# One weight sum of every second gate block on VectorE, a new order of weight loads, and term stores from ScalarE's queue

## The chip, the core and the metric

The kernel runs on one core of a Trainium2 chip. Five engines run side by side, each in its own program order: TensorE (PE) multiplies, VectorE (DVE) and ScalarE (ACT) do elementwise work, GpSimd (POOL) and SyncE (SP) issue transfers. A transfer is issued on the queue of one engine and carried by the core's 16 DMA engines. The metric is the time of one execution in microseconds (us) on the device; lower is better.

## The reference

One decoder block over 512 tokens of width 2048 in float32: an RMSNorm, one input projection, two attention mixers, an output projection, and a SwiGLU feed-forward layer with a hidden width of 5632. The change touches only the feed-forward layer, whose core is

```python
hn2 = rmsnorm(h, norm2_g[l])
h = h + (jax.nn.silu(hn2 @ w_gate[l]) * (hn2 @ w_up[l])) @ w_down[l]
return rmsnorm(h, final_g)
```

## The kernel before

**Blocks and products.** The feed-forward layer is done in 64 blocks, numbered here as in the code: 44 gate blocks (0 to 43), one for each 128 hidden columns, and 20 down blocks (44 to 63). The order stands in the table `sched`. A block holds four weight matrices of 128x1024 floats, A11, A21, A22 and A12 (512 KB each), and is computed with a seven-product scheme in place of eight plain products. The products are P1 to P7, and PE takes them in the order P1, P5, P6, P2, P7, P3, P4 (block 0 has an order of its own). Their weights are: P1 A11; P5 Y = A21 + A22; P6 Y + A11; P2 A12; P7 X = A21 + A11; P3 Y + A11 + A12; P4 A22. Signs are folded into the operands on the other side (`term`: B11, T1, T2, B21, T3, B22, T4). So four matrices are read, and four sums are formed.

**Who forms the sums.** Y and X were formed by transfers: SP loads A21 into a buffer, and then POOL issues a second transfer (line 135 of the kernel before) that reads the other matrix and adds it to the buffer. The sums of P6 and P3 are formed in Y's buffer by DVE (`comb`, line 804). For the blocks in the tuple `OWN`, DVE also forms X: A21 is loaded plainly and `comb("A11", "X")` adds A11. Before the change `OWN` held blocks 43 and 44 alone.

**Splits.** Each weight is split into a high and a low part in a narrower format before PE can use it: ACT writes the high part (`Job.first`, line 173) and DVE the low part (`Job.second`, line 176) into one of three buffers `w`. A product is 8 weight tiles with three matmuls each (lines 1015, 1016, 1017): high part by high operand, high part by low operand, low part by high operand. The low part of a weight is thus first needed by the third matmul of its product.

**Ticks.** All work is written out by hand in ticks. A tick is half a product (12 matmuls); a block has 14. For a product that PE starts at tick n, its `comb` is written at tick n-5, its high split at n-4 and its low split at n-3; within an odd tick low splits stand ahead of sums. Within a block, counted from its start, P2's low split stands at tick 3, P7's high split at 4, P7's low split and P3's sum at 5, P3's high split at 6 and P3's low split at 7. A tick is only a place in each engine's program: an engine that waits delays everything written behind it.

**Buffers and loads.** Raw weights have six buffers of 512 KB. `loads` lists all loads in order, and `load_to` issues the next one as soon as `release` has freed a buffer, so the order of the list and the places of the releases set when each load starts. A block frees its buffers at tick -1 (A11, after P6's sum), 5 (X after P7's low split, A12 after P3's sum), 7 (Y) and 9 (A22). Where DVE forms X, A11 is needed longer and is freed at tick 3.

**Evacuation and stores.** `gate` moves products out of PSUM, and `pair_terms` makes from two gate blocks the seven terms of the hidden layer, in `even1` to `even3` behind an even block and `odd1` to `odd3` behind an odd one (high parts by ACT, low parts by DVE, into the staging area in `ah` and `al`). ACT's copy of P5 (`g5`, line 1129) goes into the buffer `ft` that the previous block's `u` leaves, so it waits for the last low part that `pair_terms` makes of that `u`. After each odd block `store` writes the staged terms to DRAM, in two transfers of 896 KB, which happens while the next even block runs. They come back by `fetch` (line 1074) in the down blocks.

**Alignment.** P1's weights of every fourth block (1, 5, 9, ... and block 2) are put at another offset of the buffer `w` (`even`).

Of the kernel before, what the change touches and what calls it, by code (L numbers as in the profile page):

```python
# [11 lines left out]
F32 = mybir.dt.float32  # L12
# [10 lines left out]
FB = FF // 128  # L23
# [1 line left out]
PAIRS = 20  # L25
NCH = PAIRS // PH
FC = 2 * PAIRS
OWN = (FB - 1, FB)
PASS2 = tuple(8 * b + a for a in range(8) for b in range(2))
EPS = 1e-6  # L30
BIG = 1e30
# [44 lines left out]
def block_kernel(ctx: ExitStack, tc: tile.TileContext, xt, wst, wdn, smalls, wg, w2c, bias, ident_in, out):  # L76
# [3 lines left out]
    pe, act, dve, pool_e, sp = nc.tensor, nc.scalar, nc.vector, nc.gpsimd, nc.sync  # L80
# [27 lines left out]
    n_units = next(u for u, d in enumerate(units) if d[0] == "quad")  # L108
    loads = [(u, wst[u], None) for u in range(n_units)]
    for u in range(n_units, len(units), 4):  # L110
        a11, a21, a22, a12 = (wst[u + q] for q in range(4))
        loads += [((u, "A11"), a11, None), ((u, "Y"), a21, a22), ((u, "A12"), a12, None), ((u, "X"), a21, None if (u - n_units) // 4 in OWN else a11),
                  ((u, "A22"), a22, None)]
    loads += [(("fin", k), wdn[2 * k:2 * k + 2].rearrange("n p c -> p n c"), None) for k in range(KB // 2)]
    pools = {"raw": wp}

# [71 lines left out]
    k = 2 * units.index(("out", 0, 1))  # L188
# [43 lines left out]
    def later(n, f):  # L232
        i = len(lag)
        while i and lag[i - 1][0] > pos["half"] + n:
            i -= 1
        lag.insert(i, (pos["half"] + n, f))
# [113 lines left out]
    for k in range(KB):  # L350
        x = xc.pop(k)
# [137 lines left out]
    def evac(p, tag, scale=None, keep=False):  # L489

        t = tmp()
        if scale is None:
            dve.tensor_tensor(t, p, r1, op=OP.mult)
        else:
            dve.scalar_tensor_tensor(t, p, scale, r1, op0=OP.mult, op1=OP.mult)
        ph, pl = (MH, ML) if tag[0] == "k" else (WH, WL)
        h = placed(kvq(tag), S, ph, tag=tag + "h", name=tag + "h")
        l = placed(kvq(tag), S, pl, tag=tag + "l", name=tag + "l")
        act.activation(h, t, AF.Copy)
        dve.tensor_tensor(l, t, h.bitcast(F32), op=OP.subtract)  # L500
        return (h, l, t) if keep else (h, l)
# [212 lines left out]
    def proj_block(upto=None):  # L714
        return ps.tile([128, 512], F32, tag="proj", name="pp", bufs=2)
# [40 lines left out]
    for j in range(NH):  # L756
# [5 lines left out]
        p = proj_block()  # L762
# [8 lines left out]
        p = proj_block()  # L771
# [3 lines left out]
        p = proj_block()  # L775
        for half in range(2):
            in_unit(p, half)
        k = evac(p, "ka")
        v = V()
        queue.append(Att("dil", q, k, v, ba, None, {}, True, True, head_done(j, 0)))  # L780
        p = proj_block()
# [15 lines left out]
    def quad_jobs(u, order, even, own):  # L797

        def raw(k):
            return lambda: raws[u, k]  # L800

        def comb(k, to="Y", last=True):
            def f():
                dve.tensor_tensor(raws[u, to], raws[u, to], raws[u, k], op=OP.add)  # L804
                if last:
                    release((u, k))
            return f

        r = {"P1": Job(raw("A11"), even=even), "P5": Job(raw("Y")), "P6": Job(raw("Y"), prep=comb("A11", last=not own)),
             "P2": Job(raw("A12")), "P7": Job(raw("X"), prep=comb("A11", "X") if own else None, done=((u, "X"),)),  # L810
             "P3": Job(raw("Y"), prep=comb("A12"), done=((u, "Y"),)), "P4": Job(raw("A22"), done=((u, "A22"),))}
        return [r[p] for p in order]
# [9 lines left out]
    for i, (kind, f, m) in enumerate(sched):  # L822
        for job in quad_jobs(n_units + 4 * i, ORDER if i else ORDER0, i == 2 or i % 4 == 1, i in OWN):
            job.n = now_at // 2
# [16 lines left out]
    def out_unit(half, tag="proj"):  # L841
        p = ps.tile([128, 512], F32, tag=tag, name="pab", bufs=2)
        c = 8 - 8 * half
        run_unit([(p, ah[:, c + k, :], al[:, c + k, :], k == 0, k == 7) for k in range(8)])
        return p
# [60 lines left out]
    for nb in range(2, KB):  # L906
        while "hs" not in rest and (nb == 4 and not idle() or nb == 2 and (queue or cur["s"])):
            step()
        p = out_unit(1, ("proj", "sc", "t")[nb // 2 % 3])
# [87 lines left out]
    for i in range(KB):  # L997
        nb = PASS2[i]
        p = out_unit(0)
# [47 lines left out]
    def sub(o, a, b):  # L1047
        dve.tensor_tensor(o, a, b, op=OP.subtract)

    stage = [a[:, 12:16, :].rearrange("p a b -> p (a b)") for a in (ah, al)]  # L1050
    scr = [scp.tile([128, 14 * 1024], F32, name=f"scr{c}") for c in range(NCH)]

    def st_high(k, n, src):
        act.activation(stage[0][:, 256 * k:256 * k + 256 * n], src, AF.Copy)

    def st_low(k, n, src):
        c = slice(256 * k, 256 * k + 256 * n)
        dve.tensor_tensor(stage[1][:, c], src, stage[0][:, c].bitcast(F32), op=OP.subtract)

    def stt(o, a, b):  # L1060
        dve.scalar_tensor_tensor(o, a, -1.0, b, op0=OP.mult, op1=OP.subtract)

    def store(i):

        for x in range(2):
            d = scr[i // PH].rearrange("p (x n s c) -> p x n s c", x=2, n=7, s=PH)[:, x, :, i % PH, :]
            sp.dma_start(d, stage[x][:, :1792].bitcast(F32).rearrange("p (n c) -> p n c", c=256))

    NAMES = ("B11", "T1", "B21", "B22", "T2", "T3", "T4")

# [5 lines left out]
    def pair_terms(f, u):  # L1076

        def even1():
            st["v"] = ps.tile([128, 512], F32, tag="o", name="v")
            act.activation(st["v"][:, HI], u[:, HI], AF.Copy)  # L1080

        def even2():
            sub(u[:, HI], u[:, LO], u[:, HI])
            st_high(0, 2, u)

        def even3():
            act.activation(st["v"][:, LO], u[:, HI], AF.Copy)
            st_low(0, 2, u)

        def odd1():  # L1090
            st_high(2, 2, u)
            v = st["v"]
            sub(v[:, HI], u[:, HI], v[:, HI])
            stt(v[:, LO], v[:, LO], u[:, HI])

        def odd2():
            st_low(2, 2, u)
            v = st["v"]
            st_high(4, 2, v)
            stt(u[:, LO], v[:, LO], u[:, LO])  # L1100

        def odd3():
            st_high(6, 1, u[:, LO])
            st_low(4, 2, st["v"])
            st_low(6, 1, u[:, LO])

        for i, g in enumerate((odd1, odd2, odd3) if f % 2 else (even1, even2, even3)):
            later(i, g)
        if f % 2:
            later(5, lambda: store(f // 2))  # L1110

    def hidden(f, u):
        h, l = ah[:, 12 + f % PH, :], al[:, 12 + f % PH, :]
# [86 lines left out]
    for kind, f, m in sched:  # L1200
        order = ORDER if kind == "d" or f else ORDER0
        for i, name in enumerate(order):
            product(kind, f, m, name)
            if kind == "d":
                down(m, name)
                k = 7 * m + i
# [179 lines left out]
```

## Time and profile before

| | us |
|---|---|
| median of three runs | 2176.89 (2173.27 to 2178.32) |
| the profiled execution | 2174.71 |
| its span, first to last instruction | 2172.9 |
| start of gate block 0 | 837.0 |
| start of gate block 2 | 881.6 |
| start of down block 44 | 1718.0 |
| last down block over, last steps | from 2113.4 |

Times inside the profile count from the span's start, which is 1.8 us shorter than the execution. The median of the runs lies 2.2 us above the profiled execution. The gate blocks take 881 us of the span. Over blocks 2 to 43 (881.6 to 1718.0) DVE is busy for 633.6 us of 836.4, ACT for 419.6, and the DMA engines for 80% of the time. A matmul is shown with a modelled length of 0.28 us though the next one starts 0.11 to 0.12 us later, so PE looks busy nearly always; its pace is read from the starts.

### The profile page before, as it was taken

How to read it: one execution, taken by the hardware profiler on the slowest of the kernel's cores; microseconds unless marked ns; L12 is line 12 of the kernel's file. 1: busy time of each engine (PE TensorE's matmuls, PEld its weight loads, DVE VectorE, ACT ScalarE, POOL GpSimd, SP SyncE). 2: the span in 40 equal slices, each digit the busy share in tenths (PEclk: the TensorE clock that was granted, in tenths of full speed). 3: DMA queues.
4: the chain of work that ended last, by engine and by line, in shares of the span. 5: the costliest groups of instructions: out<-in, count | busy, mean ns of one | idle time of the engine just before them, and what ended most of it. 6: DMA issues, size and time to landing. Idle time of an engine off the chain costs nothing.

```text
span 2172.9 us, 37846 instructions
## 1 busy us (share of the span) xinstructions
PE 2146.5 (99%) x15296; PEld 2004.1 (92%) x15296; DVE 1542.1 (71%) x2510; ACT 1013.1 (47%) x1702; POOL 147.0 (7%) x172
## 2 busy tenths in 40 slices
PE   9999999999999999999999999999999999999997
PEld 8888888888888888999999999999999999999997
DVE  6755565356667588777877777777777767787875
ACT  6544444344444255554545554454545433333345
POOL 0000000000000000000000000000000000000003
PEclk9999999999999999999999999999999999999999
DMA  6442222322225335778878888787788889899862
GB/s 224 152 132 80 84 77 78 100 80 80 75 74 178 104 97 132 215 215 245 231 221 231 236 248 240 200 261 223 209 248 236 282 264 292 267 292 287 268 193 78
DMA packets 143534, 403.60 MB, mean 186 GB/s; under 512 B 12288, under 2 KB 50816, under 8 KB 143360
## 3 DMA queue, kind: packets, MB, share of 16 engines
q1 hardware_dynamic: 125072, 335.06, 43.8%
q0 software_dynamic: 18144, 66.07, 17.9%
q8 instruction: 120, 1.97, 0.4%
q14 instruction: 54, 0.44, 0.1%
q10 hardware_dynamic: 144, 0.07, 0.0%
HBM read 360.25 MB, written 40.89 MB: 185 GB/s over the span
## 4 chain that ended last, share of the span: by engine, by line
PE 76%; DMA 8%; DVE 8%; issue 4%; ACT 3%; SPq 0%; ACTq 0%; DVEq 0%; POOLq 0%
DMA raw<-in_wst_dram 8%; PE E L1015 7%; PE E L1017 7%; PE E L1016 7%; PE pp L207 7%; PE pp L209 7%; PE pp L208 7%; PE F L1017 4%; PE F L1016 4%; PE F L1015 4%; DVE w L176 3%; ACT w L173 3%; PE pab L207 3%; PE pab L209 3%; PE pab L208 3%
## 5 line engine op out<-in xcount | busy, mean ns | idle before, releaser
L173 ACT ACTIVATE w<-raw 128x1024 fp32r<-128x1024 f32 (+1 forms) x720 | 631.6, 893 | 681.9 <-DVE raw L804 278.0
L176 DVE TENSOR_TENSOR w<-raw,w 128x1024 fp32r<-128x1024 f32 (+1 forms) x720 | 727.6, 1020 | 270.9 <-ACT w L173 269.1
L1015 PE MATMUL E<-ah,w 128*128 128x256 f32 x1008 | 281.2, 279 | 5.0 <-issue 2.7
L1017 PE MATMUL E<-ah,w 128*128 128x256 f32 x1008 | 281.3, 279 | 1.3 <-DVE w L176 1.3
L1016 PE MATMUL E<-al,w 128*128 128x256 f32 x1008 | 280.5, 278 | 0.0
L207 PE MATMUL pp<-ah,w 128*128 128x512 f32 x640 | 260.6, 407 | 0.0
L209 PE MATMUL pp<-ah,w 128*128 128x512 f32 x640 | 251.0, 392 | 0.0
L208 PE MATMUL pp<-al,w 128*128 128x512 f32 x640 | 250.1, 391 | 0.0
L135 POOL DMA_DIRECT2D raw<-in_wst_dram x126 | 109.3, 868 | 1308.4 <-DMA raw<-in_wst_dram 429.4
L1015 PEld LDWEIGHTS E<-ah,w 128*128 128x128 f32 x1008 | 189.3, 188 | 6.0 <-issue 3.9
L1017 PEld LDWEIGHTS E<-ah,w 128*128 128x128 f32 x1008 | 189.4, 188 | 2.4 <-DVE w L176 2.3
L1016 PEld LDWEIGHTS E<-al,w 128*128 128x128 f32 x1008 | 189.5, 188 | 0.0
L804 DVE TENSOR_TENSOR raw<-raw 128x1024 f32<-128x1024 f32 x130 | 158.9, 1222 | 2.2
L209 PEld LDWEIGHTS pp<-ah,w 128*128 128x128 f32 x640 | 120.2, 188 | 28.3 <-DVE w L176 0.4
L1017 PE MATMUL F<-ah,w 128*128 128x256 f32 x504 | 141.9, 281 | 3.4 <-DVE w L176 3.0
L1015 PE MATMUL F<-T1h,w 128*128 128x256 f32 x504 | 141.1, 280 | 1.9 <-ACT w L173 1.9
L1017 PE MATMUL F<-T1h,w 128*128 128x256 f32 x504 | 141.4, 281 | 0.7 <-DVE w L176 0.7
L1016 PE MATMUL F<-T1l,w 128*128 128x256 f32 x504 | 141.1, 280 | 0.0
L1017 PE MATMUL E<-B11h,w 128*128 128x256 f32 x504 | 140.9, 280 | 0.0
L1016 PE MATMUL E<-B11l,w 128*128 128x256 f32 x504 | 140.8, 279 | 0.0
L1015 PE MATMUL E<-B11h,w 128*128 128x256 f32 x504 | 140.8, 279 | 0.0
L1017 PE MATMUL E<-T4h,w 128*128 128x256 f32 x504 | 140.3, 278 | 0.0
(341 smaller groups left out, 5219.5 us busy)
## 6 DMA issues: line engine op xcount, KB each, us to landing
raw<-in_wst_dram SPq DMA_DIRECT2D x454, 512.0 KB, 5.6
raw<-in_wst_dram POOLq DMA_DIRECT2D x126, 512.0 KB, 5.8
scr<-ah SPq DMA_DIRECT2D x20, 896.0 KB, 7.7
scr<-al SPq DMA_DIRECT2D x20, 896.0 KB, 10.2
ah<-scr SPq DMA_DIRECT2D x15, 512.0 KB, 7.4
al<-scr SPq DMA_DIRECT2D x15, 512.0 KB, 7.6
bias<-in_bias_dram SPq DMA_DIRECT2D x16, 320.0 KB, 3.0
xc<-in_xt_dram SPq DMA_DIRECT2D x16, 256.0 KB, 3.6
```

Source lines behind the costliest of these rows:

```text
L135: pool_e.dma_start(t, more, accum_op=OP.add)
L173: act.activation(self.h, self.src(), AF.Copy)
L176: dve.tensor_tensor(self.l, self.src(), self.h.bitcast(F32), op=OP.subtract)
L207: pe.matmul(o, wh, mh, start=start, stop=False)
L208: pe.matmul(o, wh, ml, start=False, stop=False)
L209: pe.matmul(o, wl, mh, start=False, stop=stop)
L804: dve.tensor_tensor(raws[u, to], raws[u, to], raws[u, k], op=OP.add)
L1015: pe.matmul(o, wh, mh, start=start, stop=False, skip_group_check=True)
L1016: pe.matmul(o, wh, ml, start=False, stop=False, skip_group_check=True)
L1017: pe.matmul(o, wl, mh, start=False, stop=stop, skip_group_check=True)
```

## The change

```diff
-OWN = (FB - 1, FB)
+OWN = tuple(range(1, FB, 2)) + (FB,)
...
         a11, a21, a22, a12 = (wst[u + q] for q in range(4))
-        loads += [((u, "A11"), a11, None), ((u, "Y"), a21, a22), ((u, "A12"), a12, None), ((u, "X"), a21, None if (u - n_units) // 4 in OWN else a11),
-                  ((u, "A22"), a22, None)]
+        own = (u - n_units) // 4 in OWN
+        four = {"A11": (a11, None), "Y": (a21, a22), "A12": (a12, None), "X": (a21, None if own else a11),
+                "A22": (a22, None)}
+        names = ("A11", "Y", "A12", "X", "A22") if own or u == n_units else ("Y", "A11", "X", "A12", "A22")
+        loads += [((u, k), *four[k]) for k in names]
...
-            sp.dma_start(d, stage[x][:, :1792].bitcast(F32).rearrange("p (n c) -> p n c", c=256))
+            act.dma_start(d, stage[x][:, :1792].bitcast(F32).rearrange("p (n c) -> p n c", c=256))
...
-            later(5, lambda: store(f // 2))
+            later(8, lambda: store(f // 2))
```

`OWN` now holds every odd gate block, 1 to 43, and block 44. In these 21 blocks more (1, 3, ..., 41), X is formed by DVE and its second transfer is gone. The blocks in `OWN` and block 0 keep the old order of loads. The others, which are the even gate blocks from 2 on and the down blocks from 45 on, load Y first and X ahead of A12. The stores are issued by ACT and are written three ticks later. Lines of the changed kernel are numbered three higher.

**VectorE, odd block 13**, around ticks 1 to 7. `w` is a split weight (each row of line 176 or 179 is a low split), `raw` a weight buffer: raw_9913 holds Y of block 13, raw_10015 A12, raw_10017 X, raw_9851 A11; `al` is the low half of the staging area. Before:

```order
L176 TENSOR_TENSOR w_10160<-raw_9913,w_10160 128x1024
L1048 TENSOR_TENSOR ft_9997<-ft_9997 128x256
L176 TENSOR_TENSOR w_10193<-raw_10015,w_10193 128x1024
L1058 TENSOR_TENSOR al_72<-ft_9997,ah_71 128x512
L176 TENSOR_TENSOR w_10226<-raw_10017,w_10226 128x1024
L804 TENSOR_TENSOR raw_9913<-raw_9913,raw_10015 128x1024
L176 TENSOR_TENSOR w_10261<-raw_9913,w_10261 128x1024
```

After the change:

```order
L179 TENSOR_TENSOR w_10157<-raw_9913,w_10157 128x1024
L1051 TENSOR_TENSOR ft_9997<-ft_9997 128x256
L179 TENSOR_TENSOR w_10190<-raw_10015,w_10190 128x1024
L807 TENSOR_TENSOR raw_10017<-raw_10017,raw_9851 128x1024
L1061 TENSOR_TENSOR al_72<-ft_9997,ah_71 128x512
L179 TENSOR_TENSOR w_10226<-raw_10017,w_10226 128x1024
L807 TENSOR_TENSOR raw_9913<-raw_9913,raw_10015 128x1024
L179 TENSOR_TENSOR w_10261<-raw_9913,w_10261 128x1024
```

The sum for X (raw_10017 with raw_9851) stands behind P2's low split and ahead of the low part of the staged terms.

**SyncE, from A12 of block 13 to X and A12 of block 14.** Before, the rows are A12 and X of block 13, the two stores, A22 of block 13, and A11, Y, A12 and X of block 14:

```order
L133 DMA raw_10015<-in_wst_dram 128x1024
L133 DMA raw_10017<-in_wst_dram 128x1024
L1067 DMA scr1_7123<-ah_71 128x7x256
L1067 DMA scr1_7123<-al_72 128x7x256
L133 DMA raw_10051<-in_wst_dram 128x1024
L133 DMA raw_10081<-in_wst_dram 128x1024
L133 DMA raw_10143<-in_wst_dram 128x1024
L133 DMA raw_10242<-in_wst_dram 128x1024
L133 DMA raw_10244<-in_wst_dram 128x1024
```

After the change, the rows are A12, X and A22 of block 13, then Y, A11, X and A12 of block 14:

```order
L136 DMA raw_10015<-in_wst_dram 128x1024
L136 DMA raw_10017<-in_wst_dram 128x1024
L136 DMA raw_10048<-in_wst_dram 128x1024
L136 DMA raw_10078<-in_wst_dram 128x1024
L136 DMA raw_10208<-in_wst_dram 128x1024
L136 DMA raw_10242<-in_wst_dram 128x1024
L136 DMA raw_10245<-in_wst_dram 128x1024
```

The stores have left SP. Y of block 14 (raw_10078) takes the place that A11 had, and A11 (raw_10208) now waits for the buffer that block 13's A11 leaves after the new sum.

**ScalarE, two places**, after the change (rows of line 176 are high splits here). First P4's high split of block 12, the two stores, and P1's, P5's and the next work of block 13:

```order
L176 ACTIVATE w_10062<-raw_9821 128x1024
L1070 DMA scr1_7123<-ah_71 128x7x256
L1070 DMA scr1_7123<-al_72 128x7x256
L176 ACTIVATE w_10096<-raw_9851 128x1024
L176 ACTIVATE w_10124<-raw_9913 128x1024
```

Then, in block 13, P2's high split, the high half of the staged terms (line 1057), a copy into PSUM, the copy `g5` of P5 (line 1132) and P7's high split:

```order
L176 ACTIVATE w_10190<-raw_10015 128x1024
L1057 ACTIVATE ah_71<-ft_9997 128x512
L1090 ACTIVATE v_10173<-ft_9997 128x256
L1132 ACTIVATE ft_10224<-F_10187 128x256
L176 ACTIVATE w_10226<-raw_10017 128x1024
```

Before, the same rows stood in the same order at both places, without the two stores.

## The prediction

> **What bounds the kernel now.** I read the page first. PE is busy through the whole span, so the end is set by PE's pace and by what stops PE.
>
> ```profile
> PE 2146.5 (99%) x15296; PEld 2004.1 (92%) x15296; DVE 1542.1 (71%) x2510; ACT 1013.1 (47%) x1702; POOL 147.0 (7%) x172
> ```
>
> Since a matmul's shown length overlaps the next one, I take the first row of P1 in some blocks from the timeline of PE (start, length, engine, line, tiles) and subtract.
>
> ```profile
> 881.60 0.28 PE L1015 MATMUL E<-B11h,w 128*128 128x256 f32 x1
> ...
> 1358.11 0.28 PE L1015 MATMUL E<-B11h,w 128*128 128x256 f32 x1
> ...
> 1377.89 0.28 PE L1015 MATMUL E<-B11h,w 128*128 128x256 f32 x1
> ...
> 1397.68 0.28 PE L1015 MATMUL E<-B11h,w 128*128 128x256 f32 x1
> ...
> 1717.98 0.28 PE L1015 MATMUL E<-B11h,w 128*128 128x256 f32 x1
> ...
> 1960.77 0.28 PE L1015 MATMUL E<-B11h,w 128*128 128x256 f32 x1
> ...
> 1979.81 0.28 PE L1015 MATMUL E<-B11h,w 128*128 128x256 f32 x1
> ```
>
> Block 27 takes 1397.68 - 1377.89 = 19.79 us, block 56 takes 19.04. Both run 168 matmuls without a gap, so PE has **two paces**: 117.8 ns and 113.3 ns a matmul. Blocks 2 to 43 take 1717.98 - 881.60 = 836.38; 42 blocks at the slow pace would take 831.2. Going through the product starts in the same timeline I find 49 of the 294 products at the fast pace, worth 49 x 24 x 4.45 ns = 5.2 us, so the stalls are about 836.4 - 831.2 + 5.2 = **10.4 us**. Ten odd blocks (the first is 3, the last 41) hold 7.3 of them, the even blocks 28 and 34 hold 2.5, block 16 the rest.
>
> Next the waits of PE and of ACT, over 881.6 to 1718.0 (waiter, releaser, total, times, longest):
>
> ```profile
> PE F L1017 <- DVE w L176: 3.0, 8, 0.4
> PE E L1017 <- DVE w L176: 1.3, 3, 0.5
> ...
> ACT w L173 <- DMA raw<-in_wst_dram: 42.5, 23, 4.3
> ```
>
> All that stops PE there is a low split that comes late, nearly always P3's (F, line 1017). The view counts only the visible gap; between starts such a wait costs 0.55 us and 0.1 on the next matmul. Why it is late the chain of waits shows for block 9:
>
> ```profile
> 1019.87 10.22 DMA raw<-in_wst_dram
> ...
> 1030.12 1.07 ACT w L173
> ...
> 1032.35 1.23 DVE raw L804
> ...
> 1033.60 1.07 ACT w L173
> 1034.70 1.24 DVE w L176
> ...
> 1035.98 0.39 PE F L1017
> ```
>
> The accumulating transfer of X lands at 1030.09, 9.6 us into the block. Then follow P7's high and low split, P3's sum, P3's high and low split; PE stands. In all ten odd blocks it is this chain. A short wait has a second price: in the timeline PE drops from the fast pace to the slow one at it, and comes back mostly at the odd blocks 1, 5, 9, ... whose P1 weights lie at the other offset.
>
> **Part 1: X by DVE in 21 more odd blocks.** Price and cover:
>
> ```profile
> L804 DVE TENSOR_TENSOR raw<-raw 128x1024 f32<-128x1024 f32 x85 | 103.9, 1222 | 1.4
> ...
> 1382.33 1.23 DVE L176 TENSOR_TENSOR w<-raw,w 128x1024 fp32r<-128x1024 f32 x1 [0.71 <-ACT w L173]
> 1383.47 0.69 DVE L1058 TENSOR_TENSOR al<-ft,ah 128x512 fp32r<-128x512 f32 x1
> 1386.45 1.23 DVE L176 TENSOR_TENSOR w<-raw,w 128x1024 fp32r<-128x1024 f32 x1 [2.29 <-ACT w L173]
> ...
> 1389.94 1.22 DVE L176 TENSOR_TENSOR w<-raw,w 128x1024 fp32r<-128x1024 f32 x1 [1.13 <-ACT w L173]
> ```
>
> The first row is the group of sums, the others are DVE in block 27, an odd block that isn't late: P2's low split, the staged low part, P7's low split, P3's low split. The new sum goes behind the first, where DVE has 2.29 us idle before P7's low split; 21 x 1.22 = 25.7 us of DVE are thus hidden. But they aren't free of effect: the staged low part moves 1.14 us back, and ACT waits for it.
>
> ```profile
> 1369.45 0.80 SPq L133 DMA_DIRECT2D raw<-in_wst_dram  x2
> ...
> 1384.28 0.39 ACT L1129 ACTIVATE ft<-F 128x256 f32<-128x256 f32 x1 [1.18 <-DVE al L1058]
> 1385.36 1.06 ACT L173 ACTIVATE w<-raw 128x1024 fp32r<-128x1024 f32 x1 [0.70 <-DMA raw<-in_wst_dram]
> ...
> 1365.66 0.38 ACT L1129 ACTIVATE ft<-F 128x256 f32<-128x256 f32 x1 [1.70 <-DVE al L1058]
> 1365.94 1.05 ACT L173 ACTIVATE w<-raw 128x1024 fp32r<-128x1024 f32 x1
> ```
>
> The first row is SP's issue of A12 and X. The copy of P5 starts at 1384.28 + 1.14 = 1385.42 instead, P7's high split 0.28 behind it as in block 26 (last two rows): 1385.70, 7.8 us into the block and 0.34 later than now. P3's low split then ends at 1389.94 + 1.22 + 0.34 = 1391.50. P3 starts ten ticks of 1.4135 us after 1377.89, at 1392.02, and needs it 0.24 later: **0.76 us to spare**. In the late blocks X came 8.4 to 9.6 us into the block. X is then a plain load, issued with A12 at 1369.45 or just after (first row above), 8 us before the block; even the slowest load of the stretch, 14.0 us, lands about when the sum is due, 5.6 us into it. So every odd block starts P7 at about 7.8, and none is late: -7.3 us. At the fast pace the same chain leaves about 0.4, as block 21 has now, which holds the pace.
>
> Block 1 is an exception. DVE has a backlog there from block 0, its P3 is just in time, and P7's high split starts 0.45 us later by the same sum: +0.45. Bounds: 0 and +1.2, the whole sum.
>
> **Part 2: load order.** In blocks 28 and 34 it was Y, two transfers long, that came late after stores. Y of an even block is now asked for four ticks earlier (5.6 us), X ahead of A12. The longest wait of ACT for a transfer there is 4.3 us (third row of the waits), so 5.6 covers it: -2.5 us, bounds 0 and -2.5. In return A11 of an even block is asked for 8 ticks later; that it hides is rival 2. The same order holds from block 45 on, where PE has its worst stall:
>
> ```profile
> 1740.77 0.28 PE L1015 MATMUL E<-B11h,w 128*128 128x256 f32 x1
> ...
> 1745.67 0.39 PE L1015 MATMUL F<-T1h,w 128*128 128x256 f32 x1 [1.87 <-ACT w L173]
> ...
> 1766.38 0.28 PE L1015 MATMUL E<-B11h,w 128*128 128x256 f32 x1
> ...
> 1736.86 7.59 DMA raw<-in_wst_dram
> ...
> 1728.01 4.38 SPq L133 DMA_DIRECT2D raw<-in_wst_dram  x3
> ...
> 1745.98:1752.80 6.82, 6.11 (x29) 5.87 (x28) 6.18 (x7) 2.73 (x3) 0.38 (x1) 0.50 0.45 154
> ```
>
> Block 45 takes 25.61 us, 5.8 over the slow pace: P5 waits for Y behind the fetches, and behind the wait the granted clock is 0.50 for 6.8 us (last row, a window; third number from its end). There Y was asked for at 1728.0 and is now asked for in block 43's tick 9, some 13 us earlier; A11 gets the late place, and lands about where Y's first half did, at 1736.3, 0.9 after P1's high split wants it and with 3 us to spare. So both go: -5.6, with bounds 0 and -5.8. The Trainium skill ("TensorE: Matmul & The Clock Gate", Part 1: The HAM clock gate) has the clock halved only after a whole idle window of about 3.4 us. Here the longest gap is 1.87 us and the clock fell all the same, so I follow the row; by the page some 2.5 us would not belong to the stall and would stay, and the sum below would be 2161.3 in place of 2158.8.
>
> **Part 3: stores from ACT.**
>
> ```profile
> 1372.49 1.06 ACT L173 ACTIVATE w<-raw 128x1024 fp32r<-128x1024 f32 x1 [1.05 <-issue]
> ...
> L1067 SPq DMA_DIRECT2D scr<-ah x20: 424/426/1086, 894.2 to 1650.7; - x20
> L1067 SPq DMA_DIRECT2D scr<-al x20: 377/556/906, 894.7 to 1651.2; - x20
> ...
> scr<-ah SPq DMA_DIRECT2D x20, 896.0 KB, 7.7
> scr<-al SPq DMA_DIRECT2D x20, 896.0 KB, 10.2
> ...
> DMA to landing us min/median/max: 3.6/6.2/14.0
> ...
> q0 software_dynamic: 11942, 43.49, 30.7%
> ```
>
> The issues (second and third row: shortest, median and longest in ns) take about 1 us a pair. On ACT they stand ahead of the next block's P1 high split, where ACT is idle for 1.05 us (first row, block 26): hidden, and if not, that split ends at 1373.55 and P1 starts at 1377.89. Three ticks later in the program changes little, since SP already waited until then. Value 0; bounds as rival 1. The accumulating transfers of this stretch (last row) take 30.7% of the DMA engines' time; 20 fewer take 7.5 points off the 80%. That helps all landings, and I count nothing for it.
>
> **Pace.** With odd blocks on time, an odd block that gets the fast pace keeps it into the next even block, which loses it at P3: in block 26 P7's high split starts at 7.8, and at the fast pace blocks 22 and 38 had 0.17 us to spare there and fell back. Six of ten such blocks got it now. Six times 11 products make 7.0 us in place of 5.2, less 0.9 for even blocks up to 16 whose P3 is then late: about -1, bounds +4 and -5.
>
> **Sum**: 2174.71 - 7.3 - 2.5 - 5.6 - 1 + 0.45 = 2158.8 on the profiled execution; the median of the runs lies 2.2 above that execution and the lowest run 1.4 below it, so 2161 and 2157. I take **2160**.
>
> **Rivals.** (1) The stores land later. Their staged low part is overwritten 6.7 us into the odd block (5.6 before), 13.8 us after the issue; the medians are 7.7 and 10.2 us. With 0.76 to spare, each us past 14.6 us stalls 20 odd blocks: at 15.1 us, +10, **2170**. Against it: fewer bytes in flight. For it: the stores no longer stand ahead of the loads in one queue. The Trainium skill ("DMA: Bandwidth & Descriptors", Queues, rings and completion order) says that each DMA engine takes turns among its queues packet by packet; by it the stores share with loads that stood behind them, and land later than now.
>
> (2) **Slower**: A11 of an even block is late. It is asked for after the new sum, 6.8 us into the odd block, and must land by 19.8 + 0.24 - 2.4 (both splits) = 17.6: within 10.5 us. The median load takes 6.2, the slowest, behind stores, 14.0. Each us past 10.5 stalls 20 blocks, and from 11.3 us the gain is gone; at 11.9, 28 us, **2188**.
>
> (3) P3's margin holds in even blocks too and PE stays at the fast pace: 836.4 - 801 = 35 us off, **2135**. Nothing in the change shortens the even block's chain.
>
> (4) It doesn't do what it says: DVE is too far behind in odd blocks and P3 stays late. Then blocks 28, 34 and 45 alone pay, at most: **2169**, and no change at all if block 45 doesn't.
>
> **Chances**: forecast 0.60 (2154 to 2166), (1) 0.13, (2) 0.10, (3) with smaller gains of pace 0.08, (4) 0.09. The range 2150 to 2174 leaves out (2), most of (3) and the tail of (4). One measurement can tell about 0.2%, 4.4 us, from no change. Faster by more: 0.60 + 0.08 + most of (1) and half of (4) = 0.79; within it 0.11; slower 0.10.
>
> **What would show it.** Right: P7's high split 7.8 us into odd blocks with no wait for a transfer, no wait of PE for P3 in odd blocks, block 45 near 19.8 and the clock 1.00 in it, 151 sums by DVE. Wrong: ACT waiting for a transfer ahead of P1's split in even blocks (rival 2), DVE or ACT waiting for the stores at the staged parts (rival 1), a granted clock of 0.50 in block 45.

## The result, and the profile after

| | before | after |
|---|---|---|
| median of four runs (us) | 2177.53 | 2153.05 |
| lowest and highest | 2173.27, 2178.32 | 2147.22, 2155.11 |
| the profiled execution | 2174.71 | 2155.11 |

The ratio is 0.9887, with a 95% interval of 0.9864 to 0.9911: 24 us or 1.1% faster. Between the profiled executions it is 19.6 us, and the forecast for that execution was 15.9 (2158.8).

First the busy times from the page after, and the group of sums by DVE (line 807):

```profile
PE 2134.8 (99%) x15296; PEld 1996.0 (93%) x15296; DVE 1567.5 (73%) x2531; ACT 1012.2 (47%) x1702; POOL 128.9 (6%) x151
...
L807 DVE TENSOR_TENSOR raw<-raw 128x1024 f32<-128x1024 f32 x151 | 184.6, 1222 | 2.2
```

The 21 sums are there (151, before 130), at the 1.22 us that was forecast, and PE is busy 11.7 us less at the same number of matmuls. The timeline of PE after gives the starts of blocks 0, 2, 22, 23, 44, 45, 46 and 56, the first rows of P1:

```profile
837.21 0.28 PE L1018 MATMUL a<-B11h,w 128*128 128x256 f32 x1
...
883.16 0.28 PE L1018 MATMUL E<-B11h,w 128*128 128x256 f32 x1
...
1275.72 0.28 PE L1018 MATMUL E<-B11h,w 128*128 128x256 f32 x1
...
1294.76 0.28 PE L1018 MATMUL E<-B11h,w 128*128 128x256 f32 x1
...
1705.04 0.28 PE L1018 MATMUL E<-B11h,w 128*128 128x256 f32 x1
...
1728.92 0.28 PE L1018 MATMUL E<-B11h,w 128*128 128x256 f32 x1
...
1748.76 0.28 PE L1018 MATMUL E<-B11h,w 128*128 128x256 f32 x1
...
1941.71 0.28 PE L1018 MATMUL E<-B11h,w 128*128 128x256 f32 x1
```

Subtracting, and comparing with the rows of before:

| stretch | before | after | difference | forecast |
|---|---|---|---|---|
| blocks 0 and 1 | 44.6 | 45.95 | +1.3 | +0.45 |
| blocks 2 to 43 | 836.4 | 821.9 | -14.5 | -10.8 |
| block 44 | 22.8 | 23.9 | +1.1 | 0 |
| block 45 | 25.6 | 19.84 | -5.8 | -5.6 |
| blocks 46 to 55 | 194.4 | 192.95 | -1.4 | 0 |
| sum | | | -19.3 | -15.9 |

Block 22, an even one, takes 19.04 us: it keeps the fast pace, which the forecast let end at P3 of an even block. In blocks 2 to 43 I count 102 products at the fast pace (49 before). The 53 more are worth 53 x 24 x 4.45 ns = 5.7 us, so the stalls gave about 14.5 - 5.7 = 8.8 us.

The waits of ACT after, over blocks 2 to 43 (the two longest groups of that list):

```profile
ACT w L176 <- DVE raw L807: 166.0, 85, 2.2
ACT ft L1132 <- DVE al L1061: 78.4, 39, 2.6
```

No row of the list names a weight transfer any more (42.5 us before), and the list of PE's waits for the same stretch is empty. Block 27 shows how an odd block runs now: the block's start on PE, DVE's sum for X and the staged low part, then ACT's copy of P5 and P7's high split, from the timeline:

```profile
1371.49 0.28 PE L1018 MATMUL E<-B11h,w 128*128 128x256 f32 x1
...
1377.07 1.22 DVE L807 TENSOR_TENSOR raw<-raw 128x1024 f32<-128x1024 f32 x1
1378.21 0.69 DVE L1061 TENSOR_TENSOR al<-ft,ah 128x512 fp32r<-128x512 f32 x1
...
1379.01 0.38 ACT L1132 ACTIVATE ft<-F 128x256 f32<-128x256 f32 x1 [2.32 <-DVE al L1061]
1379.29 1.05 ACT L176 ACTIVATE w<-raw 128x1024 fp32r<-128x1024 f32 x1
```

The sum stands ahead of the staged low part, ACT's copy waits for that part, and P7's high split follows 7.80 us into the block: the forecast's figure. In block 45 the window from its start to its end has a granted clock of 1.00 (third number from the end):

```profile
1728.90:1748.80 19.90, 19.90 (x171) 19.90 (x170) 16.12 (x18) 7.44 (x7) 1.72 (x2) 1.00 1.00 248
```

So every sign that the prediction named is there. That doesn't yet say which part of the change did it.

### The profile page after: what moved, and what is told of

The parts are those of the page before. It is cut to its first block, busy times and chain, and to the rows that moved or that the text cites. A ratio compares the mean times of both kernels' runs of the same rounds, so it can differ in the third digit from the quotient of the medians.

```text
span 2153.3 us, 37787 instructions
## 1 busy us (share of the span) xinstructions
PE 2134.8 (99%) x15296; PEld 1996.0 (93%) x15296; DVE 1567.5 (73%) x2531; ACT 1012.2 (47%) x1702; POOL 128.9 (6%) x151
## 4 chain that ended last, share of the span: by engine, by line
PE 92%; DVE 4%; ACT 2%; issue 1%; DMA 1%; ACTq 0%; DVEq 0%; POOLq 0%; SPq 0%
PE E L1020 10%; PE E L1018 10%; PE E L1019 10%; PE pp L210 7%; PE pp L212 7%; PE pp L211 7%; PE F L1020 5%; PE F L1019 5%; PE F L1018 5%; PE pab L210 3%; PE pab L211 3%; PE pab L212 3%; PE G L1020 2%; PE G L1019 2%; PE G L1018 2%
## 5 line engine op out<-in xcount | busy, mean ns | idle before, releaser
L807 DVE TENSOR_TENSOR raw<-raw 128x1024 f32<-128x1024 f32 x151 | 184.6, 1222 | 2.2
L138 POOL DMA_DIRECT2D raw<-in_wst_dram x105 | 91.1, 868 | 1303.9 <-DMA raw<-in_wst_dram 498.2
L1020 PE MATMUL E<-T4h,w 128*128 128x256 f32 x504 | 140.2, 278 | 0.0
L1019 PE MATMUL E<-T4l,w 128*128 128x256 f32 x504 | 140.1, 278 | 0.0
L1019 PE MATMUL F<-al,w 128*128 128x256 f32 x504 | 140.1, 278 | 0.0
L1018 PE MATMUL E<-T4h,w 128*128 128x256 f32 x504 | 140.1, 278 | 0.0
## 6 DMA issues: line engine op xcount, KB each, us to landing
scr<-al ACTq DMA_DIRECT2D x20, 896.0 KB, 12.7
```

The source lines that it names most:

```text
L138: pool_e.dma_start(t, more, accum_op=OP.add)
L1018: pe.matmul(o, wh, mh, start=start, stop=False, skip_group_check=True)
L1019: pe.matmul(o, wh, ml, start=False, stop=False, skip_group_check=True)
L1020: pe.matmul(o, wl, mh, start=False, stop=stop, skip_group_check=True)
```

## The experiments

The change has three parts: the sum (S), the order of loads (O) and the stores from ACT (A). I ran all eight combinations of them, then six kernels on the pace and on what is left. A ratio is always to the kernel before on the same chip.

| parts | median (us) | ratio, 95% interval |
|---|---|---|
| none | 2174 to 2178 | 1 |
| S | 2208.81 | 1.0158, 1.0135 to 1.0182 |
| A | 2202.58 | 1.0135, 1.0109 to 1.0161 |
| S + A | 2206.92 | 1.0150, 1.0128 to 1.0171 |
| O | 2154.13 | 0.9900, 0.9881 to 0.9919 |
| O + A | 2241.68 | 1.0294, 1.0262 to 1.0327 |
| O + S | 2151.89 | 0.9893, 0.9874 to 0.9911 |
| O + S + A (the change) | 2153.05 | 0.9887, 0.9864 to 0.9911 |

Two of the three parts make the kernel slower when made alone, by 27 to 35 us. The third alone gives the whole gain.

**The sum alone.**

```diff
-OWN = (FB - 1, FB)
+OWN = tuple(range(1, FB, 2)) + (FB,)
```

> The kernel before with one part of the change: OWN holds every odd gate block, so DVE forms X there. Loads keep the old order, stores stay on SP. Theory A (each stall has its own cause): the stalls at P3 in odd blocks go (7.3 us in blocks 2 to 43) and more products keep the fast pace (about 5 us), blocks 28 and 34 may still wait for Y (2.5 us) and block 45 stays at 25.6 us; about 2165 us beside 2177 before. Rival B (the loads gain because the stores left SP's queue, and the sum is only the price paid): odd blocks keep part of their stalls, at most 5 us off, 2172 or more.

It took 2208.81 us: neither theory. Odd blocks are mended, as theory A had it, but all even gate blocks stall. Requests and waits around block 14, an even one: SP's request of Y, POOL's second transfer of Y, the block's start, and ACT's high split of P5, which waits for Y.

```profile
1116.04 0.33 SPq L133 DMA_DIRECT2D raw<-in_wst_dram  x1
...
1120.39 0.86 POOL L135 DMA_DIRECT2D raw<-in_wst_dram  x1 [23.49 <-DMA raw<-in_wst_dram]
...
1128.31 0.28 PE L1015 MATMUL E<-B11h,w 128*128 128x256 f32 x1
...
1128.70 1.06 ACT L173 ACTIVATE w<-raw 128x1024 fp32r<-128x1024 f32 x1 [4.24 <-DMA raw<-in_wst_dram]
```

The same request and second transfer in the kernel before, and its block 14's start:

```profile
1102.28 0.33 SPq L133 DMA_DIRECT2D raw<-in_wst_dram  x1
...
1111.69 0.86 POOL L135 DMA_DIRECT2D raw<-in_wst_dram  x1 [10.71 <-ACT ft L1132]
...
1121.28 0.28 PE L1015 MATMUL E<-B11h,w 128*128 128x256 f32 x1
```

Before, Y was asked for 19.0 us ahead of the block; now 12.3 ahead. The sum needs A11 of the odd block until tick 3 where it used to be freed at tick -1, and in the old order the load that gets this buffer is Y of the next block, the one that takes two transfers. ACT stands 4.24 us for it, and P6, P2, P7 and P3, whose splits are queued behind, are late in turn (127 to 151 ns a matmul from start to start in place of 118).

**The change without its order.** Here every block has the tuple `("A11", "Y", "A12", "X", "A22")` again.

> The changed kernel with the old order of loads in all blocks (sum by DVE and stores from ACT stay). Theory A: block 45 goes back to 25.6 us (+5.8), with the clock at 0.50 behind its wait, and some even blocks wait for Y again (0 to +2.5); 2159 to 2161 us beside 2153 of the changed kernel. Rival B (with 20 accumulating transfers fewer and the stores in another queue Y lands in time anyway): block 45 stays near 20 and the time within 2 us of the changed kernel's.

2206.92 us (the median of five runs; a sixth took 12190.34 and is left out): the same picture. Even blocks wait for Y, and block 45 takes 25.5 us. Theory A had block 45 right (+5.6) and missed the even blocks, since it took A11's longer life for granted.

**The change with the stores on SP.**

```diff
-            act.dma_start(d, stage[x][:, :1792].bitcast(F32).rearrange("p (n c) -> p n c", c=256))
+            sp.dma_start(d, stage[x][:, :1792].bitcast(F32).rearrange("p (n c) -> p n c", c=256))
...
-            later(8, lambda: store(f // 2))
+            later(5, lambda: store(f // 2))
```

> The changed kernel with the stores issued by SP at the old place (sum and new order stay). Theory A: the stores' queue is worth nothing, as forecast: 2153 us, within 3. Rival B (the stores stand ahead of the loads of the next even block in SP's queue): the loads issued behind them land late again, ACT waits for Y or A11 in even blocks, and 3 to 10 us of the gain are lost, 2156 to 2163.

2151.89 us: theory A, the queue of the stores is worth nothing in the changed kernel.

**The change without its sum.** `OWN` is as before, and the order goes by block number.

> The changed kernel with X of odd blocks formed by the accumulating transfer again (order of loads by block as in the change, stores from ACT). Theory A: X lands 8.4 to 9.6 us into some odd blocks again, P3's low split is late there (+7.3 us) and the fast pace is lost again (about +5): about 2165 us. Rival B (the room made by the stores' new queue lets X land in time): no P3 wait in odd blocks, within 3 us of the changed kernel's 2153.

2241.68 us: far from both. The longest wait of DVE for a transfer (waiter, releaser, total, times, longest):

```profile
DVE al L1062 <- DMA scr<-al: 90.7, 19, 7.4
```

The second stores on its page (the last number is the median time to landing):

```profile
scr<-al ACTq DMA_DIRECT2D x20, 896.0 KB, 18.3
```

And from the timeline around odd block 13 the second store's issue, the two second transfers that follow (X of block 13, Y of block 14) and the staged low part:

```profile
1110.73 0.59 ACTq L1071 DMA_DIRECT2D scr<-al  x1
...
1117.14 0.86 POOL L139 DMA_DIRECT2D raw<-in_wst_dram  x1 [10.86 <-DVE ft L1147]
1121.94 0.86 POOL L139 DMA_DIRECT2D raw<-in_wst_dram  x1 [3.94 <-DMA raw<-in_wst_dram]
...
1129.89 0.69 DVE L1062 TENSOR_TENSOR al<-ft,ah 128x512 fp32r<-128x512 f32 x1 [5.76 <-DMA scr<-al]
```

This is the prediction's first rival, in another kernel: the second store lands 19 us after its issue, DVE stands 5.76 us for it, ACT's copy of P5 waits for DVE, and P7 and P3 are late. In the changed kernel the median is 12.7 us, and this wait sums to 0.2 us. The first of the two transfers is the one that the sum takes away.

**The order alone.**

```diff
+        old = i in OWN or i == 0 or i < FB and i % 2
+        names = ("A11", "Y", "A12", "X", "A22") if old else ("Y", "A11", "X", "A12", "A22")
```

> The kernel before with the new order of loads alone (even gate blocks and down blocks from 45 load Y first, X ahead of A12); sums by transfer, stores on SP at the old place. Theory A (the run without the sum lost its time to the second store, which landed 18.3 us after its issue from ACT's queue beside two accumulating transfers, so that the staged low part waited): with the stores on SP again they land at about 10 us, no staged part waits, blocks 28, 34 and 45 are mended and odd blocks keep their stalls at P3; 2166 to 2170 us beside 2175 before. Rival B (the order itself is what doesn't fit the transfers that form X): 2200 us or more.

2154.13 us, 12 better than theory A and the same as the whole change. X of the odd blocks still comes by transfer, but in time. Block 9 in this kernel (request of X, its second transfer, the block's start, ACT's high split of P7):

```profile
1010.54 0.33 SPq L137 DMA_DIRECT2D raw<-in_wst_dram  x1
...
1016.31 0.87 POOL L139 DMA_DIRECT2D raw<-in_wst_dram  x1 [9.42 <-DMA raw<-in_wst_dram]
...
1019.06 0.28 PE L1019 MATMUL E<-B11h,w 128*128 128x256 f32 x1
...
1026.13 1.07 ACT L177 ACTIVATE w<-raw 128x1024 fp32r<-128x1024 f32 x1 [0.26 <-DMA raw<-in_wst_dram]
```

The request and the block's start in the kernel before; its second transfer (1019.87) and high split (1030.12) stand in the prediction's chain of waits:

```profile
1012.79 1.07 SPq L133 DMA_DIRECT2D raw<-in_wst_dram  x1
...
1020.48 0.28 PE L1015 MATMUL E<-B11h,w 128*128 128x256 f32 x1
```

X is asked for 8.5 us ahead of the block in place of 7.7, its second transfer starts 2.75 ahead in place of 0.6, and P7's high split starts 7.1 us in, where it was 9.6. So an order that is changed only in even blocks reaches into the odd ones: X and A12 of the even block leave their buffers in the other sequence, and the requests of the next block wait for those buffers. In the kernel before, A12 of block 9 is requested at 1012.37, right behind P3's sum of block 8 on DVE, and X 0.42 us behind it. Here A12 goes at 1009.41, behind P7's low split of block 8, and X 1.1 us later, at the end of P3's sum; X's first transfer then lands in 5.1 us in place of 6.5. No run takes this apart from Y's earlier place.

**The stores alone.**

> The kernel before with the stores issued by ACT three ticks later, and nothing else: the last of the eight combinations of the three parts. Theory A (as in the run without the sum: the transfer that forms X of an odd block runs beside the stores and holds the second one back to 18 us, so that the staged low part waits for it): 2220 us or more beside 2175. Rival B (in that run the new order of loads had to be there too): within 10 us of 2175.

2202.58 us, between the two theories. The second store lands at 13.2 us (median), in time in most blocks: DVE waits for it 8 times, 21.9 us in all. X is late as well. Around block 13 the timeline has the block's start, X's second transfer and P7's high split, which waits for it:

```profile
1107.17 0.28 PE L1015 MATMUL E<-B11h,w 128*128 128x256 f32 x1
...
1107.46 0.86 POOL L135 DMA_DIRECT2D raw<-in_wst_dram  x1 [12.36 <-DVE w L176]
...
1117.10 1.06 ACT L173 ACTIVATE w<-raw 128x1024 fp32r<-128x1024 f32 x1 [2.45 <-DMA raw<-in_wst_dram]
```

The transfer starts 0.3 us into the block (0.7 ahead of block 13 in the kernel before), the split 9.9 us into it, and P3 is late in every odd block from 3 to 41. Against 19.79 us a block, the eight odd blocks in which DVE waits for the store take 16.2 us more, the other twelve 8.2; how the two causes share the eight is not shown.

So stores that leave SP's queue land later themselves (13.2 us in place of 10.2) and hold X back as well. They are not issued later: the second store goes out 11.9 us into the even block (median), and went out 13.1 us into it before. The Trainium skill's rule that the prediction quoted ("DMA: Bandwidth & Descriptors", Queues, rings and completion order) has the queues take turns; these numbers agree with it.

**The pace: the copy behind the split.** ACT's copy of P5 waits for the staged low part, and P7's high split stood behind it.

```diff
-        if name in ("P1", "P5", "P6") and (f, name) != (1, "P5"):
+        if name in ("P1", "P6"):
```

> The changed kernel with ACT's copy of P5 (g5) written behind P7's high split instead of ahead of it, in all gate blocks. Theory A (the fast pace is lost in even blocks because P3's low split has only 0.17 us to spare there, and that margin hangs on this copy, which waits for the staged low part): P7's high split starts about 6 to 7 us into a block instead of 7.8, P3 has about 1 us to spare, PE keeps the fast pace from block 2 to 43, these take about 802 us instead of 821.8, in all 2133 to 2137 us beside 2153. Rival B (the pace falls back for another reason, or the copy delays the low parts of the next block): within 4 us of 2153.

2135.61 us, ratio 0.9813 (0.9797 to 0.9829): theory A. Starts of blocks 2, 26 and 44 in it, and in block 26 P7's high split ahead of the copy:

```profile
883.14 0.28 PE L1018 MATMUL E<-B11h,w 128*128 128x256 f32 x1
...
1341.21 0.28 PE L1018 MATMUL E<-B11h,w 128*128 128x256 f32 x1
...
1684.57 0.28 PE L1018 MATMUL E<-B11h,w 128*128 128x256 f32 x1
...
1347.00 1.05 ACT L176 ACTIVATE w<-raw 128x1024 fp32r<-128x1024 f32 x1
1348.74 0.39 ACT L1132 ACTIVATE ft<-F 128x256 f32<-128x256 f32 x1 [0.69 <-DVE al L1061]
```

The split starts 5.8 us into the block, and blocks 2 to 43 take 801.4 us, every product but the P1s at the other offset (120 ns) at 113.3 ns.

**The pace: no other offset, and twice as many.** First `even` is False in every block:

> The changed kernel with P1's weights at the ordinary offset in every block. Theory A (the other offset in P1 is what lets PE go over to the fast pace): PE stays at the slow pace in all gate and down blocks; blocks 2 to 43 take about 831 us instead of 821.8 and blocks 49 to 63 about 11 us more; 2171 to 2175 us. Rival B (PE finds the fast pace by itself): within 4 us of 2153.

2176.2 us (ten of eleven runs within 2174.9 to 2177.4, one 2160.25): theory A, but for that one run, of which there is no trace. The starts of blocks 2 and 44 are 831.0 us apart, 42 times 19.79, though nothing stalls PE there:

```profile
883.86 0.28 PE L1018 MATMUL E<-B11h,w 128*128 128x256 f32 x1
...
1714.89 0.28 PE L1018 MATMUL E<-B11h,w 128*128 128x256 f32 x1
```

Then the other offset in every odd block (`i == 2 or i % 2 == 1`):

> The changed kernel with P1's weights at the other offset in every odd block, not in every fourth. Theory A (each such P1 is a chance of about two in three to go over to the fast pace): blocks 3, 7, 11, 15 and so on get it too, about 0.6 to 1.2 us each, some 8 us in all, 2143 to 2147 us. Rival B (whether a block takes the fast pace hangs on what else runs then, not on the offset): within 4 us of 2153.

2149.22 us, ratio 0.9878 (0.9860 to 0.9895): neither theory. The time lies 2 us above theory A's range and inside rival B's, and the interval overlaps that of the changed kernel. The trace bears out the mechanism of theory A, not its worth. Of 16 odd gate blocks that were reached at the slow pace 11 went over to the fast one, the two in three of the theory, and 186 products of blocks 2 to 43 are fast (102 in the changed kernel). But even blocks still lose the pace at P3, so that a block earns little.

**What the sum is worth when the copy is out of the way.** The order alone, with the copy behind the split.

> The kernel before with the new order of loads and the copy of P5 behind P7's high split; no sum for X by DVE, stores on SP. It asks what the sum is worth. Theory A (with the copy out of the way the odd blocks hang on X, which its transfer delivers 7 to 8 us into the block and the sum by DVE delivers at 6.9): even blocks keep the fast pace, odd blocks lose it at P3, whose low split is late there by up to 0.5 us; 2140 to 2150 us beside 2135.6 with the sum. Rival B (the sum is worth nothing once the order is right): 2134 to 2138.

2134.75 us, ratio 0.9816 (0.9797 to 0.9835): rival B. X's second transfer, too, starts earlier here (2.5 to 4.3 us ahead of odd blocks 5 to 11), and by the medians the sum by DVE is worth nothing here either. The profiled execution shows theory A's loss once: in block 31 X's second transfer starts only 1.1 us ahead and P7's split 8.3 us into the block, P3 is late, and blocks 31 to 36 run slow, 4.3 us in all. That execution took 2141.42 us, the other three 2132.85 to 2136.29. Whether the sum guards against such a loss, four runs don't settle.

**Block 44.** The changed kernel with the copy behind the split and

```diff
-        names = ("A11", "Y", "A12", "X", "A22") if own or u == n_units else ("Y", "A11", "X", "A12", "A22")
+        names = ("A11", "Y", "A12", "X", "A22") if own and u < n_units + 4 * FB or u == n_units else ("Y", "A11", "X", "A12", "A22")
...
-        for job in quad_jobs(n_units + 4 * i, ORDER if i else ORDER0, i == 2 or i % 4 == 1, i in OWN):
+        for job in quad_jobs(n_units + 4 * i, ORDER if i else ORDER0, i in (2, 3, 45, 46, 47), i in OWN):
```

> The changed kernel with the copy of P5 behind P7's high split, the new order of loads in block 44 too, and P1's other offset in blocks 2, 3, 45, 46 and 47 alone. Theory A (in block 44 P5 waits for Y, which is asked for 12.9 us ahead of the block and lands after it has begun; each P1 at the other offset costs 0.15 us where the pace is fast already): Y lands in time, block 44 falls from 24.5 to about 21 us, blocks 46 to 48 are fast, 15 P1s are cheaper; 2126 to 2131 us. Rival B (block 44 waits for the operands that are fetched there, not for Y): block 44 stays above 23.5 us, 2131 to 2134.

2128.97 us, ratio 0.9783 (0.9768 to 0.9798), the fastest of all: theory A. Starts of blocks 44, 45 and 46 in it:

```profile
1683.34 0.28 PE L1018 MATMUL E<-B11h,w 128*128 128x256 f32 x1
...
1703.34 0.28 PE L1018 MATMUL E<-B11h,w 128*128 128x256 f32 x1
...
1724.18 0.28 PE L1018 MATMUL E<-B11h,w 128*128 128x256 f32 x1
```

Block 44 takes 20.0 us (24.5 without its new order), and block 45 pays 1.0 of it (20.84).

**Rival 2's price.** In the change A11 of even blocks moves one more place back, `("Y", "X", "A11", "A12", "A22")`.

> The changed kernel with A11 of even blocks third in the order, behind X. It moves A11's request about 4.4 us back (from 12.9 us ahead of the even block to 8.5) and tests the second rival's price. In the changed kernel A11 lands 7.4 to 9.0 us ahead of the block and P1's low split needs it by about 2.2 ahead. Theory A (rival 2 had its mechanism right, and has 5 us of room): A11 lands 3 to 4 us ahead, P1's high split is 1.5 to 2.5 us late but nothing stalls for long; 2150 to 2158. Rival B (ACT, waiting for A11, holds back what stands behind it): even blocks stall by 0.5 us or more each, 2163 or more.

2159.25 us, ratio 0.9923 (0.9910 to 0.9936). The waits of PE and, below, ACT's for a weight transfer in blocks 2 to 43:

```profile
PE F L1020 <- DVE w L179: 1.7, 5, 0.5
PE E L1020 <- DVE w L179: 0.8, 2, 0.5
...
ACT w L176 <- DMA raw<-in_wst_dram: 19.3, 11, 2.5
```

ACT waits for a transfer 11 times and PE stands 7 times; the medians are 6 us apart, 1 more than theory A allowed. The mechanism exists, and the change keeps clear of it.

## Why the prediction was right, and where its reasons were not

**Time and sign.** 2153.05 us is 7 below the 2160 on record and inside the range; the likeliest case came about, with no stall in odd blocks and none for Y.

**Part 1, "every odd block starts P7 at about 7.8, and none is late: -7.3".** True of the changed kernel (7.80). As a price of the sum it failed: alone it costs 35 us. Alone it does mend the odd blocks, but so does the order: with the order alone X still comes by transfer, and no odd block from 3 to 41 takes more than 19.84 us. So beside the order the sum adds nothing, and that its figure came true is luck. The prediction worked out DVE's 1.22 us and its place, but not that `comb` now holds A11 four ticks longer and what load then waits for that buffer. The front of the text names the later release; the sum gave it no term.

**Part 2, the order, "-2.5" and "-5.6".** Block 45 came out at -5.8, and the clock stayed at 1.00. But the part was mis-sized as a whole: alone it is worth 20 us, and beside the sum 57 (2208.81 against 2151.89), since it gives Y an early place (asked for 23.9 us ahead of block 14) and hands the late buffer to A11, which needs one transfer and has room. In the text this stood as a risk (rival 2), not as what makes part 1 possible.

**Part 3, the stores, "value 0".** Right in the changed kernel (2151.89 with SP). The bounds were taken from rival 1, at most 10 us; without the sum the same edit costs 88 us (2154.13 against 2241.68), and alone 27. The forecast held because the sum takes away the transfer that runs beside the second store; beside the sum, in the old order too, the edit changes nothing (2208.81 without it, 2206.92 with it).

**Pace, "about -1, bounds +4 and -5".** The term that was mis-sized most: 53 more products at the fast pace, -5.7 us, past its bound. The prediction let the fast pace end at P3 of each even block; blocks 22 and 34 kept it. Another 1.4 us came the same way behind block 50.

**Block 1, "+0.45".** +1.3, just past its upper bound of +1.2, the length of one sum. In the profiled execution after the change P6 of block 1 takes 4.46 us in place of 2.93, because the granted clock is 0.50 for 3.4 us there (rows under "The clock" below); the prediction had no term for that. The sum costs about as much without it: in the run of the sum alone the clock stays at 1.00 there, P2, P7 and P3 are late, and block 1 takes 23.28 us, 1.1 more than before. **Block 44**, to which no term was given, takes 1.1 us more; there, too, the clock is 0.50 for 3.4 us, and P6 takes 4.15 us in place of 2.91.

**The rivals.** Stores later: 12.7 us for 10.2, but with 0.2 us of waiting. A11 late: not in the change; 6 us when pushed. (Its room was 17.6 - 6.8 = 10.8 us, where the text goes on with 10.5; nothing hangs on it.) The fast pace throughout: not by this change, but it is what the copy's place gives, and 801.4 us is the forecast's own figure (801). DVE too far behind: no.

## What to carry to other kernels

An edit's price holds what it keeps as well as what it does: ask how much longer each buffer lives and which load stands next for it, since here that was 35 us, where the work itself, 1.22 us a block, was hidden. Parts that are made together may each be the condition of another; price them alone and in pairs before a gain is put down to one of them. And where the list of waits is empty, compare the pace all the same: in the changed kernel it still held 20 us (821.9 against 801.4) with no wait of PE listed.

## What the runs showed that was not expected

- **Two paces of PE, and weights' offset.** With no stall at all PE runs 42 blocks in 831.0 us or in 801.4. Without the other offset in P1 it stays at 117.8 ns a matmul in the profiled execution (one run of eleven was 16 us faster than the others), with it PE goes over to 113.3 in 11 of 16 cases. The fast pace mostly ends at a P3 whose low split comes late or just in time: in the changed kernel P3's third matmul starts 0.27 to 0.31 us late in blocks 6, 10 and 14, and in 24, 26 and 38 no delay is visible. With the other offset in every odd block, block 14 kept the pace over such a delay of 0.31. Why the offset does it is open.
- **The clock.** In the change without its order, block 45 has one gap of 1.6 us and one of 0.8, by the waits of PE:

```profile
PE F L1018 <- ACT w L176: 1.6, 1, 1.6
PE F L1020 <- DVE w L179: 0.8, 1, 0.8
```

The window behind the first gap has a granted clock of 0.53 (third number from the end):

```profile
1777.90:1784.70 6.80, 6.04 (x29) 5.84 (x29) 6.16 (x7) 2.68 (x3) 0.23 (x1) 0.53 0.48 157
```

The page of the Trainium skill that the prediction cited, "TensorE: Matmul & The Clock Gate", Part 1: The HAM clock gate, asks for an idle window of about 3.4 us; the row decides.

The length of a gap alone doesn't settle it either. In block 1 PE stands 1.86 us ahead of P6 both before and after the change. The window behind that gap, first in the kernel before, then in the changed one:

```profile
868.00:871.40 3.40, 3.40 (x31) 3.40 (x30) 2.34 (x4) 2.05 (x5) 0.00 (x0) 1.00 0.75 137
...
868.00:871.40 3.40, 3.40 (x19) 3.40 (x18) 2.70 (x3) 0.91 (x3) 0.00 (x0) 0.50 0.00 0
```

In block 44 a gap of 2.18 us ahead of P6 is followed by 3.4 us at 0.50 after the change, one of 1.98 us before it by none. What decides is open.

- **A store in its own queue.** The second store of 896 KB lands after 10.2 us (medians) in the loads' queue with X's second transfer beside it (kernel before) and after 10.1 without (the sum alone). In ACT's queue it lands after 12.7 us (changed kernel) and 13.5 (the change without its order) though X has no second transfer there, after 13.2 where X has one (the stores alone), and after 18.3 where the second transfers of X and Y both run beside it (without the sum).
